# Three spacers that move a two-layer hybrid decoder's matmul operands to multiples of 128 bytes

## The chip, the cores and the metric

The program runs on one core of a Trainium2 chip, in one launch. The metric is device time in microseconds (us): the median of several executions. A partition is one of the 128 rows of the core's on-chip memory; a tile takes the same range of bytes in each of its partitions, and "position" below means the address of a tile's first byte in a partition, modulo 128.

## The reference

Two decoder layers over 256 tokens of 2048 channels. Each layer normalises and modulates its input, multiplies it with one wide matrix, feeds three mixers (a forgetting attention, a sparse attention, a state-space scan), gates and projects each of them, and adds up:

```python
u = rms_norm(x, norm_w) * (1.0 + scale[:, None, :]) + shift[:, None, :]
proj = jnp.dot(u, w_in)                       # 2048 x 18776 columns
...
merged = (gates[:, :, 0] * jnp.dot(y_fox, w_o_fox)
          + gates[:, :, 1] * jnp.dot(y_dsa, w_o_dsa)
          + gates[:, :, 2] * jnp.dot(y_ssd, w_o_ssd))
out = jnp.dot(merged, w_out)
return x + gate[:, None, :] * out
```

Shift, scale and gate come from a product of a second input `c` with `w_ada` (2048 x 6144 for each layer). Everything is float32.

## The kernel before

Weights come in halves of 128 x 1024 float32 (0.5 MB, one transfer of the SP queue into one of seven buffers `raw`). Of each half ScalarE makes a high part `wh` (L175, type float32r) and VectorE the rest `wl` (L176). Activations are split in the same way: `uh` and `ul` are the normalised input, `yh0`, `yl0`, `yh1`, `yl1` the two attentions' outputs, `ysh` and `ysl` the state-space mixer's, `mh` and `ml` the merged sum. Each product of two matrices is then three float32r products into one PSUM bank: high by high, low by high, high by low.

There are two shapes. In `feat` (L213 to L215) a 128 x 128 block of weights is stationary and 256 tokens of an activation stream past it: 256 columns to a product, and new stationary weights for each. In `tok_half` (L180 to L182) 128 tokens are stationary and 512 columns of weights stream past: 15 blocks in each layer, 8 halves a block, 12 products a half, 2880 in all.

TensorE runs in the order in which the program emits its products, so the order is the source's. A clock of ticks, one at each half, places the mixers' small products (plain float32: logits, transposes with `ident`, state-space sums) between the large ones. The first layer starts with ten blocks in `tok_half` form while the modulation `w_ada` is loaded and reduced on VectorE (L229); more of `w_ada` is loaded later beside the other weights, by tick.

Each tile is put by a pool that fills a partition from one end: `const`, `wp` (`raw`, `wh`, `wl`), `up` (`uh`, `ul`), `small`, then the mixers' pools stand one behind the other from the left; `yp`, and what is opened behind it (`ysp` with `ysh` and `ysl`), come from the right end. Sizes are rounded up to 32 bytes. In the built programs this gives these addresses in a partition (modulo 128 in brackets; the two modulo 256 behind the slash):

```
tile          before                 after
wh (first)    65248 (96) / 224       65280 (0) / 0
wl (first)    81632 (96) / 224       81664 (0) / 0
uh            93920 (96) / 224       93952 (0) / 0
ul           110304 (96) / 224      110336 (0) / 0
yh0, mh      137120 (32) / 160      137216 (0) / 0
ml           153504 (32) / 160      153600 (0) / 0
ysh          174944 (96) /  96      174848 (0) / 0
ysl          191328 (96) /  96      191232 (0) / 0
raw (first)   36576 (96) / 224       36608 (0) / 0
qT, kT              (32)                   (0)
dqT, dkT            (96)                   (0)
crep          16512  (0)             16544 (32)
ones, ident         (64)                  (96)
```

All buffers of `wh`, `wl` and `raw` lie 4096 bytes apart, and the blocks inside a tile 512, 1024 or 2048 bytes, so that each operand of a large product starts at its tile's position.

Of the kernel before, what the change touches and what calls it, by code (L numbers as in the profile page):

```python
# [10 lines left out]
F32 = mybir.dt.float32  # L11
# [5 lines left out]
PSUM = bass.MemoryType.PSUM  # L17
# [5 lines left out]
BIG = -1e30  # L23
# [32 lines left out]
# modulation: (layer, blocks, first tick, ticks a tile)  # L56
ADA = ((0, range(8, 12), 212, 1.8), (1, range(8), 270, 1.9), (1, range(8, 12), 600, 4.0))
# start: steps by which the modulation runs ahead of its use, loads of x after which a tile of it is loaded
AHEAD, EARLY = 1, (1,)
# ticks between dependent products of a mixer, by layer  # L60
# [9 lines left out]
class Net:  # L70
    def __init__(self, ctx, tc, xT, c, pos, inv, par, w_ada, w_tm, w_ts, w_sm, w_od, outT):
        self.tc, self.nc = tc, tc.nc
        self.xT, self.c, self.pos, self.inv, self.par = xT, c, pos, inv, par
        self.w_ada, self.w_tm, self.w_ts, self.w_sm, self.w_od, self.outT = w_ada, w_tm, w_ts, w_sm, w_od, outT
        pool = lambda **k: ctx.enter_context(tc.tile_pool(**k))
        self.const = pool(name="const", bufs=1)
        self.wp = pool(name="wp", bufs=1)
        self.up = pool(name="up", bufs=1)
        self.small = pool(name="small", bufs=1)
        self.mm = pool(name="mm", bufs=4, space=PSUM)  # L80
        self.mx = pool(name="mx", bufs=4, space=PSUM)
        self.dram = pool(name="dram", bufs=1, space=DRAM)
        self.ada_queue = []
        self.front = -1000000
        self.nticks = 0
        self.lanes = [[], [], []]
        # TensorE issues in emission order: ticks place the mixers' products between the projections'
        ctx.enter_context(tc.manual_schedule(engines={mybir.EngineType.PE}))

# [21 lines left out]
    def spawn(self, n, gen, *after):  # L111
        """queue a mixer's steps; it starts when the jobs it follows have been emitted"""
        job = Layer()
        job.gen, job.after, job.done = gen, after, False
        self.lanes[n].append(job)
        return job
# [17 lines left out]
    @contextmanager  # L134
    def first(self):
        """what the weights' stream needs goes before everything else, in its own order"""
        tc = self.tc
        outer, tc.cur_priority = tc.cur_priority, self.front
        yield
        self.front, tc.cur_priority = tc.cur_priority, outer  # L140
# [4 lines left out]
    def rsqrt(self, out, ss, scale, eps, tag):  # L145
        """out = (ss * scale + eps) ** -0.5"""
        nc = self.nc
        shape = list(ss.shape)
        x, y, t = [self.st(shape, tag + n) for n in ("_x", "_y", "_t")]
        i = t.bitcast(I32)  # L150
        nc.vector.tensor_scalar(x, ss, scale, eps, op0=OP.mult, op1=OP.add)
        nc.vector.tensor_scalar(i, x.bitcast(I32), 1, None, op0=OP.logical_shift_right)
        nc.vector.tensor_scalar(y.bitcast(I32), i, -1, 0x5F3759DF, op0=OP.mult, op1=OP.add)
        for n in range(3):
            nc.vector.tensor_mul(t, y, y)
            nc.vector.scalar_tensor_tensor(t, t, -0.5, x, op0=OP.mult, op1=OP.mult)
            nc.vector.scalar_tensor_tensor(out if n == 2 else y, t, 1.5, y, op0=OP.add, op1=OP.mult)

# [6 lines left out]
    def half(self, src):  # L165
        """half a piece, as high and low parts"""
        with self.first():
            r = self.raw(src)
            h = self.wp.tile([P, 1024], F32R, tag="wh", name="wh", bufs=NWH)
            l = self.wp.tile([P, 1024], F32R, tag="wl", name="wl", bufs=NWL)  # L170
            self.split(h, l, r)
        return h, l
# [11 lines left out]
    def tok_half(self, out, src, k, k0, k1):  # L184
        """two k tiles x 512 columns, activations stationary"""
        h, l = self.half(src)
        for i in range(2):
            c = slice(i * 512, i * 512 + 512)
            for th in range(2):
                s = slice(th * P, th * P + P)  # L190
                self.three(out[th], self.uh[:, k + i, s], self.ul[:, k + i, s], h[:, c], l[:, c], k + i == k0, k + i == k1)

    def tok_group(self, blocks):
        """out[b][th] is a bank [token, 512 columns]"""
        out = [[self.mmbank() for _ in range(2)] for _ in blocks]
        for k in range(0, KT, 2):
            for b, blk in enumerate(blocks):
                src = self.w_tm[self.l, blk, k // 2]
                self.tok_half(out[b], src, k, 0, KT - 1)
                self.tick()  # L200
        return out

    def feat(self, src, ah=None, al=None, nk=KT):
        """weights stationary: a bank half [128 columns, 256 tokens]"""
# [16 lines left out]
    def ada_raw(self, l, blk, n, r=None):  # L221
        """modulation: half of the sum for the feature tile blk * 4 + n // 2; after every second tile the pair is put together"""
# [35 lines left out]
    def load(self, x, ssq, *tmp):  # L258
        """what the first products wait for: silu of c on all partitions, x and its sum of squares"""
# [97 lines left out]
    def rstd_row(self, ssq):  # L357
        """1 / rms of each token, along the free axis of every partition"""
        nc = self.nc
        ps = self.pbank()  # L360
        for th in range(2):
            nc.tensor.matmul(ps[:, th:th + 1], lhsT=ssq[:, th * P:th * P + P], rhs=self.ones[:, :1], start=True, stop=True)
        rs = self.st([P, 2], "rsu")
        self.rsqrt(rs, ps[:, :2], 1.0 / DM, EPS, "nu")
        pr = self.pbank()
        for th in range(2):
            nc.tensor.matmul(pr[:, th * P:th * P + P], lhsT=rs[:, th:th + 1].to_broadcast([P, P]), rhs=self.ident, start=True, stop=True)
        return pr
# [5 lines left out]
    def u_tile(self, l, k, t):  # L374
        """u = x * A * rstd + shift, as high and low parts"""
# [13 lines left out]
    def start(self, blocks, x, ssq, row, raws, got):  # L389
        """first layer: the modulation arrives by pairs of feature tiles; the first products over each four tiles  # L390
        run as soon as their part of u is there, and add up in SBUF (those of the first two blocks in PSUM)"""
# [64 lines left out]
    def head_rstd(self, t, nh, pool):  # L456
        """1 / rms of each head of t [token, 2, nh * 128]"""
# [11 lines left out]
    def to_heads(self, dst, h0, t, c0, scale=None):  # L469
        """two 128-column blocks of token-major t -> dst[:, h0:h0+2, tokens]"""  # L470
# [11 lines left out]
    def rope(self, v, half, c0, pool):  # L482
        """v [token, 2, heads, dims]: rotate the first 2 * half dims"""
# [32 lines left out]
    def g_small(self, ps, sm, dtt, par, lay, D, pool):  # L516
        """softplus of sdt, log sigmoid of ff, their cumulative sums"""
# [33 lines left out]
        # forget gate: cumulative sums, token-major and as rows (those of the keys)  # L551
# [7 lines left out]
        # state-space decays: cumulative sums by chunk, token-major and as rows  # L559
# [18 lines left out]
    def g_heads(self, n, logits, vals, dst, pool):  # L578
        """causal attention, a head a tick: logits, then softmax and its transpose, then the product with the values"""
# [73 lines left out]
    def g_index(self, iqT, ikT, sm, acc, pool):  # L653
        """scores of the indexer; acc becomes 0 at the selected causal keys and BIG elsewhere"""
# [50 lines left out]
    def gate_y(self, name, y, pool):  # L705
        """y *= 2 * silu(gate); y came with a factor of a half"""
# [10 lines left out]
    def layer(self, l):  # L717
# [3 lines left out]
        # right: y of the attentions, temporaries of both; left: one mixer's operands  # L721
# [13 lines left out]
        D.Fq = yp.tile([P, 2, 8], F32, name="Fq")  # L735
        vp, close_v = self.pool("vp", "left")
# [12 lines left out]
        if l == 0:  # L749
            # x lies where the transposed heads come later  # L750
# [3 lines left out]
        def got(name, j=0, t=None):  # L754
            """a block of projections is there, token-major: the next steps of its mixer"""
# [5 lines left out]
            elif name == "iq":  # L761
                # indexer queries, transposed, lie where the attention's output comes later
# [138 lines left out]
    def conv(self, f, dst, sp):  # L901
        """causal depthwise convolution over 128 channels, then SiLU"""
# [112 lines left out]
    def g_norm(self, l, g, gates, y, sp, S):  # L1015
        """gate and group norm, transposed"""
# [42 lines left out]
def _ada_raws(w):  # L1059
    """w [2048, 6144] by feature tile and half of k, transposed"""  # L1060
# [3 lines left out]
def _pack(i):  # L1064
# [12 lines left out]
    # halves [128, 1024] of pieces: two k tiles x 512 columns, or eight k tiles x 128 columns  # L1077
# [29 lines left out]
```

## Time and profile before

| what | value |
|---|---|
| three timed runs | 2459.23, 2460.9, 2467.44 us; median 2460.9 |
| span of the profiled execution (its own time) | 2465.1 us, 4.2 us over the median |
| TensorE busy | 2418.5 us, 98% of the span, 17256 products |
| VectorE, ScalarE busy | 1752.3 us (71%), 1195.9 us (49%) |
| read from HBM | 520.74 MB, 213 GB/s over the span |
| mean granted TensorE clock | 0.997 |

A product's time in the trace is modelled at its end, so that the times of neighbours overlap: one that is shown with 0.28 us may be followed 0.12 us later by the next. What a product costs in a dense stretch is the step from its start to the next one's start, and that is what the timeline's first column gives. The granted clock is 1.00 where TensorE runs at its upper level, 2.4 GHz.

### The profile page before, as it was taken

How to read it: one execution, taken by the hardware profiler on the slowest of the kernel's cores; microseconds unless marked ns; L12 is line 12 of the kernel's file. 1: busy time of each engine (PE TensorE's matmuls, PEld its weight loads, DVE VectorE, ACT ScalarE, POOL GpSimd, SP SyncE). 2: the span in 40 equal slices, each digit the busy share in tenths (PEclk: the TensorE clock that was granted, in tenths of full speed). 3: DMA queues.
4: the chain of work that ended last, by engine and by line, in shares of the span. 5: the costliest groups of instructions: out<-in, count | busy, mean ns of one | idle time of the engine just before them, and what ended most of it. 6: DMA issues, size and time to landing. Idle time of an engine off the chain costs nothing.

```text
span 2465.1 us, 43733 instructions
## 1 busy us (share of the span) xinstructions
PE 2418.5 (98%) x17256; PEld 2247.5 (91%) x17256; DVE 1752.3 (71%) x3109; ACT 1195.9 (49%) x1932; POOL 1.8 (0%) x11
## 2 busy tenths in 40 slices
PE   6999999999999999999989999999999999999999
PEld 4778799998899999999978877999999999999999
DVE  8899978777766777776775567767776655666554
ACT  4535656555544444343344655555555444444443
POOL 0000000000000000000000000000000000000000
PEclk9999999999999999999999999999999999999999
DMA  9998434544468888788865544544544667776564
GB/s 341 331 328 290 146 120 138 161 157 159 157 214 281 289 281 288 271 276 269 306 205 184 188 138 146 177 152 153 161 155 162 227 229 238 231 233 229 187 214 155
DMA packets 145216, 527.79 MB, mean 214 GB/s; under 512 B 16369, under 2 KB 16881, under 8 KB 145009
## 3 DMA queue, kind: packets, MB, share of 16 engines
q1 hardware_dynamic: 145010, 525.00, 63.4%
q8 instruction: 135, 2.21, 0.4%
q14 instruction: 71, 0.58, 0.1%
HBM read 520.74 MB, written 4.19 MB: 213 GB/s over the span
## 4 chain that ended last, share of the span: by engine, by line
PE 89%; DVE 5%; DMA 4%; issue 1%; ACT 0%; SPq 0%; DVEq 0%
PE pm L213 19%; PE pm L215 19%; PE pm L214 19%; PE pm L180 8%; PE pm L182 8%; PE pm L181 8%; DMA raw<-w_ada 3%; DVE wl L176 2%; DVE raw L229 2%; PE px L987 1%; PE px L475 1%; PE px L609 1%; PE px L996 1%; DMA raw<-w_od 1%; PE held L181 0%
## 5 line engine op out<-in xcount | busy, mean ns | idle before, releaser
L175 ACT CAST wh<-raw 128x1024 fp32r<-128x1024 f32 x788 | 825.4, 1050 | 1002.0 <-PE pm L214 547.5
L176 DVE TENSOR_TENSOR wl<-raw,wh 128x1024 fp32r<-128x1024 f32 x788 | 959.9, 1222 | 344.1 <-PE pm L215 152.9
L213 PE MATMUL pm<-uh,wh 128*128 128x256 f32 x2848 | 816.5, 287 | 0.0
L215 PE MATMUL pm<-uh,wl 128*128 128x256 f32 x2848 | 805.7, 283 | 1.1 <-DVE wl L176 1.1
L214 PE MATMUL pm<-ul,wh 128*128 128x256 f32 x2848 | 805.0, 283 | 0.0
L213 PEld LDWEIGHTS pm<-uh,wh 128*128 128x128 f32 x2848 | 545.1, 191 | 5.2 <-issue 3.9
L214 PEld LDWEIGHTS pm<-ul,wh 128*128 128x128 f32 x2848 | 545.3, 191 | 2.1 <-issue 1.9
L215 PEld LDWEIGHTS pm<-uh,wl 128*128 128x128 f32 x2848 | 545.1, 191 | 1.6 <-DVE wl L176 1.5
L180 PE MATMUL pm<-wh,uh 128*128 128x512 f32 x896 | 361.1, 403 | 1.1 <-ACT uh L378 1.1
L182 PE MATMUL pm<-wl,uh 128*128 128x512 f32 x896 | 352.1, 393 | 6.9 <-DVE wl L176 6.8
L229 DVE SCALAR_TENSOR_TENSOR raw<-raw,crep 128x1024 f32<-128x1024 f32 x192 | 234.0, 1223 | 174.8 <-DMA raw<-w_ada 174.8
L181 PE MATMUL pm<-wh,ul 128*128 128x512 f32 x896 | 350.7, 391 | 0.0
L182 PEld LDWEIGHTS pm<-wl,uh 128*128 128x128 f32 x896 | 169.0, 189 | 46.2 <-DVE wl L176 10.2
L180 PEld LDWEIGHTS pm<-wh,uh 128*128 128x128 f32 x896 | 169.1, 189 | 39.9 <-issue 3.0
L181 PEld LDWEIGHTS pm<-wh,ul 128*128 128x128 f32 x896 | 169.3, 189 | 35.3 <-issue 1.9
L215 PE MATMUL pm<-mh,wl 128*128 128x256 f32 x512 | 142.5, 278 | 5.2 <-DVE wl L176 4.9
L215 PE MATMUL pm<-ysh,wl 128*128 128x256 f32 x512 | 144.7, 283 | 1.2 <-DVE wl L176 1.2
L214 PE MATMUL pm<-ysl,wh 128*128 128x256 f32 x512 | 144.2, 282 | 0.0
L213 PE MATMUL pm<-ysh,wh 128*128 128x256 f32 x512 | 144.1, 281 | 0.0
L214 PE MATMUL pm<-ml,wh 128*128 128x256 f32 x512 | 141.6, 277 | 1.4 <-DVE ml L176 1.4
L213 PE MATMUL pm<-yh,wh 128*128 128x256 f32 x512 | 142.0, 277 | 0.0
L214 PE MATMUL pm<-yl,wh 128*128 128x256 f32 x512 | 141.8, 277 | 0.0
(315 smaller groups left out, 2814.9 us busy)
## 6 DMA issues: line engine op xcount, KB each, us to landing
raw<-w_ts SPq DMA_DIRECT2D x352, 512.0 KB, 3.9
raw<-w_tm SPq DMA_DIRECT2D x240, 512.0 KB, 3.6
raw<-w_ada SPq DMA_DIRECT2D x192, 512.0 KB, 4.6
raw<-w_od SPq DMA_DIRECT2D x192, 512.0 KB, 4.5
raw<-w_sm SPq DMA_DIRECT2D x4, 512.0 KB, 4.7
xr<-xT SPq DMA_DIRECT2D x4, 512.0 KB, 7.0
x<-xn SPq DMA_DIRECT2D x4, 512.0 KB, 6.4
xr<-x SPq DMA_DIRECT2D x4, 512.0 KB, 6.1
```

Of the source, the lines that this page charges most:

```text
L175: self.nc.scalar.copy(h, src)
L176: self.nc.vector.tensor_sub(l, src, h.bitcast(F32))
L180: mm(ps, lhsT=ah, rhs=bh, start=start, stop=False)
L181: mm(ps, lhsT=al, rhs=bh, start=False, stop=False)
L182: mm(ps, lhsT=ah, rhs=bl, start=False, stop=stop)
L213: mm(ps, lhsT=h[:, c], rhs=ah[:, k, :], start=k == 0, stop=False)
L214: mm(ps, lhsT=h[:, c], rhs=al[:, k, :], start=False, stop=False)
L215: mm(ps, lhsT=l[:, c], rhs=ah[:, k, :], start=False, stop=k == nk - 1)
L229: nc.vector.scalar_tensor_tensor(r, r, 0.5, self.crep[:, n % 2 * 1024:n % 2 * 1024 + 1024], op0=OP.mult, op1=OP.mult, accum_out=m.part[:, ...
L475: nc.tensor.transpose(ps[:, j * SEQ + th * P:j * SEQ + th * P + P], t[:, th, c0 + j * P:c0 + j * P + P], self.ident)
L609: nc.tensor.matmul(po[:, :SEQ], lhsT=v[:, 0], rhs=pT[:, :SEQ], start=True, stop=False)
L987: nc.tensor.matmul(pd[:, c * 256 + o % 256:c * 256 + o % 256 + 64], lhsT=dec[:, i, c, :], rhs=xd[:, c, o:o + 64], start=True, stop=True)
```

## The change

Before `wp` a spacer of 32 bytes is put into `const`, which moves everything that stands behind it on the left (weights, `uh`, `ul`, and with a second spacer of 64 bytes in `small` all the mixers' pools). A spacer of 96 bytes at the end of `yp` moves what comes from the right. Each spacer is a tile that GpSimd sets to zero once, so that it is allocated; nothing reads it. The rest of the diff takes comments out of the source and moves line numbers (the function `half` and the products have the same text).

```diff
         self.const = pool(name="const", bufs=1)
+        self.pad(self.const, 32)
         self.wp = pool(name="wp", bufs=1)
         self.up = pool(name="up", bufs=1)
         self.small = pool(name="small", bufs=1)
+        self.pad(self.small, 64)
...
+    def pad(self, pool, nbytes):
+
+        t = pool.tile([P, nbytes // 4], F32, name="pad")
+        self.nc.gpsimd.memset(t, 0.0)
...
         D.Fq = yp.tile([P, 2, 8], F32, name="Fq")
+        self.pad(yp, 96)
```

The order of instructions on TensorE, ScalarE and the SP queue is the same. On GpSimd, at the start of the program, these rows stood before (`ident` is the unit matrix for the transposes, `logf` a table of the forgetting attention):

```order
masks.py:197 MEMSET ident 128x128
L544 MEMSET logf 128x80
masks.py:199 ISA
masks.py:199 AFFINE_SELECT ident<-ident 128x128
L299 AFFINE_SELECT tri<-tri 128x128
L304 AFFINE_SELECT msk<-msk 128x128 x2
L544 MEMSET logf 128x80
```

And these stand there now:

```order
masks.py:197 MEMSET ident 128x128
L128 MEMSET pad 128x8
L128 MEMSET pad 128x16
L128 MEMSET pad 128x24
L551 MEMSET logf 128x80
masks.py:199 ISA
masks.py:199 AFFINE_SELECT ident<-ident 128x128
L306 AFFINE_SELECT tri<-tri 128x128
L311 AFFINE_SELECT msk<-msk 128x128 x2
L128 MEMSET pad 128x24
L551 MEMSET logf 128x80
```

Three settings of a spacer now stand ahead of the one that finishes `ident`, and a fourth, that of the second layer's `yp`, ahead of the second layer's `logf`. On VectorE two small copies of `ident` into `hot` change places with one scaling, all within the first set-up.

## Rows read from the trace of the kernel before

**Rows 1.** The page: busy time of each engine, and the transfers' share in slices.

```profile
PE 2418.5 (98%) x17256; PEld 2247.5 (91%) x17256; DVE 1752.3 (71%) x3109; ACT 1195.9 (49%) x1932; POOL 1.8 (0%) x11
DMA  9998434544468888788865544544544667776564
```

**Rows 2.** The page: the chain that ended last, by engine.

```profile
PE 89%; DVE 5%; DMA 4%; issue 1%; ACT 0%; SPq 0%; DVEq 0%
```

**Rows 3.** The page: groups of large products, moving operand first; busy, mean, idle before.

```profile
L213 PE MATMUL pm<-uh,wh 128*128 128x256 f32 x2848 | 816.5, 287 | 0.0
...
L180 PE MATMUL pm<-wh,uh 128*128 128x512 f32 x896 | 361.1, 403 | 1.1 <-ACT uh L378 1.1
...
L213 PE MATMUL pm<-yh,wh 128*128 128x256 f32 x512 | 142.0, 277 | 0.0
```

**Rows 4.** Timeline of TensorE, `uh` and `ul` moving: start, duration, instruction.

```profile
710.77 0.28 PE L214 MATMUL pm<-ul,wh 128*128 128x256 f32 x1
...
711.85 0.28 PE L214 MATMUL pm<-ul,wh 128*128 128x256 f32 x1
```

**Rows 5.** The same view, `yh` and `yl`, then `mh` and `ml` moving.

```profile
705.29 0.28 PE L215 MATMUL pm<-yh,wl 128*128 128x256 f32 x1
...
706.32 0.28 PE L215 MATMUL pm<-yh,wl 128*128 128x256 f32 x1
...
2399.76 0.28 PE L214 MATMUL pm<-ml,wh 128*128 128x256 f32 x1
...
2400.89 0.28 PE L215 MATMUL pm<-mh,wl 128*128 128x256 f32 x1
```

**Rows 6.** The same view, `ysh` and `ysl` moving.

```profile
2197.78 0.28 PE L214 MATMUL pm<-ysl,wh 128*128 128x256 f32 x1
...
2198.85 0.28 PE L214 MATMUL pm<-ysl,wh 128*128 128x256 f32 x1
```

**Rows 7.** The same view, 512 columns of weights moving.

```profile
1319.79 0.39 PE L181 MATMUL pm<-wh,ul 128*128 128x512 f32 x1
...
1320.70 0.39 PE L182 MATMUL pm<-wl,uh 128*128 128x512 f32 x1
```

**Rows 8.** Groups by shape: two plain float32 products of 256 columns.

```profile
L626 PE MATMUL px<-kT,qT 128*128 128x256 f32 x32 | 9.6, 380 | 0.0
L700 PE MATMUL px<-dkT,dqT 128*128 128x256 f32 x32 | 9.6, 380 | 0.0
```

**Rows 9.** The chain about 244 us: start, length, what.

```profile
244.40 0.87 PE px L475 x8
```

**Rows 10.** Windows: length, busy of each engine, granted clock, DMA share, GB/s.

```profile
30.00:210.00 180.00, 172.47 (x730) 139.46 (x731) 166.59 (x271) 77.23 (x94) 0.00 (x0) 0.99 0.92 328
...
700.00:1025.00 325.00, 325.00 (x2752) 324.78 (x2751) 232.29 (x332) 138.96 (x161) 0.00 (x0) 1.00 0.82 277
1025.00:1255.00 230.00, 221.12 (x1851) 217.76 (x1850) 167.06 (x262) 91.62 (x115) 0.00 (x0) 1.00 0.84 282
...
1900.00:2465.00 565.00, 562.03 (x4779) 561.83 (x4777) 329.14 (x413) 236.08 (x272) 0.00 (x0) 1.00 0.65 215
```

**Rows 11.** Waits of TensorE: in total, times, longest.

```profile
PE pm L215 <- DVE wl L176: 7.1, 10, 2.1
PE pm L182 <- DVE wl L176: 6.8, 5, 1.9
```

**Rows 12.** The chain from 1095 to 1135 us.

```profile
1096.19 5.80 DMA raw<-w_ada
...
1103.27 4.33 DMA raw<-w_ada
...
1108.89 4.65 DMA raw<-w_ada
```

**Rows 13.** Groups by shape: two VectorE operations, and one setting on GpSimd.

```profile
L176 DVE TENSOR_TENSOR wl<-raw,wh 128x1024 fp32r<-128x1024 f32 x788 | 959.9, 1222 | 344.1 <-PE pm L215 152.9 <-PE pm L182 112.5 <-issue 61.2
...
L229 DVE SCALAR_TENSOR_TENSOR raw<-raw,crep 128x1024 f32<-128x1024 f32 x192 | 234.0, 1223 | 174.8 <-DMA raw<-w_ada 174.8
...
L544 POOL MEMSET logf<- 128x80 f32 x2 | 0.3, 166 | 264.3 <-PE px L558 264.3
```

## The prediction

> **What bounds the kernel now.** I read the page's busy times first: TensorE is busy 98% of the span, VectorE 71% [rows 1]. The chain that ended last agrees: 89% of it is TensorE, 5% VectorE, 4% transfers [rows 2]. So nearly all of the time is the number of products times the step from one to the next, and the view that counts is the timeline's column of starts.
>
> There the steps differ by the moving tile, although shape, type and granted clock (1.00, the level of 2.4 GHz) are the same. Ten starts with `uh` and `ul` span 1.08 us: 120.0 ns a product [rows 4]. With `yh` and `yl` nine steps take 1.03 us, 114.4 ns; with `mh` and `ml` ten take 1.13 us, 113.0 ns [rows 5]. With `ysh` and `ysl` nine take 1.07 us, 118.9 ns [rows 6]. Where 512 columns of weights stream, four steps take 0.91 us, 227.5 ns [rows 7]. One column per clock would be 256 / 2.4 = 106.7 ns and 512 / 2.4 = 213.3 ns. The excess is thus some 13 ns for `uh`, as much for 512 columns (14), 12 for `ysh`, and 6 to 8 for `yh` and `mh`. It is paid per product, not per column.
>
> Against the table of addresses: what costs 12 to 14 ns more starts 96 bytes into its 128, what costs 6 to 8 starts 32 bytes into it. Two stretches are not TensorE's alone: up to about 230 us transfers run at 328 GB/s and a share of 0.92 with VectorE busy 166.59 of 180 us, and from 1025 to 1255 us (282 GB/s) TensorE has gaps [rows 10].
>
> **The change part by part.** *Price of an aligned product.* No row has one. Along the line from 96 bytes (120.0) through 32 bytes (mean of 114.4 and 113.0: 113.7) position 0 is at 113.7 - (120.0 - 113.7) / 2 = 110.5 ns; by `mh` alone it is 109.5. I take 110. The lower bound is 106.7, the upper the best step seen, 113.0. Each product also loads 128 columns of weights: eight transposes, each with such a load, take 0.87 us, 108.75 ns each [rows 9], so loads come fast enough for 110. For 512 columns I take the same 10 ns off, 217.5, between 213.3 and 220.5.
>
> The Trainium skill has a price for a warm stream, in "TensorE: Matmul & The Clock Gate", section "Back-to-back issue gap": columns over 2.4 plus 2.5 ns, 109.2 and 215.8 here. No stretch of this trace shows it, and by it the sum below would be 144 us instead of 130.
>
> *The sum.* `uh` and `ul`: 3 x 2848 products [rows 3] x 10.0 = 85.4 us. `ysh` and `ysl`: 3 x 512 x 8.9 = 13.7 (the groups of `ysh`, `yh` and `mh` all have 512). `yh`: 1536 x 4.4 = 6.8; `mh`: 1536 x 3.0 = 4.6. Products of 512 columns: 2880 by the listing, less the 960 of the ten starting blocks, 1920 x 10.0 = 19.2. Together 129.7 us. With the lower bounds: 13.3 x 8544 + 12.2 x 1536 + 7.7 x 1536 + 6.3 x 1536 + 14.2 x 1920 ns = 181 us; with the upper ones: 7.0 x 8544 + 5.9 x 1536 + 1.4 x 1536 + 7.0 x 1920 ns = 85 us.
>
> *What does not become shorter.* The starting blocks I give nothing: 960 x 10 ns would be 9.6 us, but there transfers and VectorE set the pace [rows 10]. If transfers gained from their new places in `raw`, VectorE's 166.59 of 180 us would leave 13 us at most; the trace shows no transfer to another position of `raw`, so I take nothing.
>
> From 1025 to 1255 us the chain goes through one transfer of `w_ada` after another (5.80, 4.33 and 4.65 us within 20 us [rows 12]). The potential in it is about 530 products of `uh` x 10.0 + 530 of `ysh` x 8.9 + 768 of `mh` x 3.0 ns = 12.3 us (1851 products in that window [rows 10], split by the order of the source); as TensorE is still busy 221 of 230 us there, I take half of it off, 6 us. Between 700 and 1025 us transfers have a share of 0.82 at 277 GB/s; a step shorter by a fifteenth makes that 0.88, under the 0.92 of the start, so the gain holds. From 1900 us on the share is 0.65 and nothing is near [rows 10].
>
> TensorE waits for `wl` 15 times for 13.9 us [rows 11]; with weights used up faster a wait of 2 us can come more often, 4 us off. What is late next is VectorE's split: 1222 ns a half against 24 x 110 ns = 2.6 us, with its other work 71% of the span before and about 75% after.
>
> *Moved positions with no price.* `ident` and `ones` go from 64 to 96. Plain float32 products take no notice: `kT` at 32 and `dkT` at 96 both show 380 ns [rows 8]. Nor does VectorE: `crep` at 0 and `wh` at 96 as second operand give 1223 and 1222 ns [rows 13]. The four settings of spacers are shorter than the 166 ns of `logf` [rows 13], and GpSimd is busy 1.8 us in all [rows 1]. The three ahead of `ident` delay it by at most 0.5 us, hidden behind the loading of `x`; without that cover they would cost those 0.5 us.
>
> So 129.7 - 6 - 4 = 119.7 us off the profiled execution's 2465.1: 2345. That execution was 4.2 us over the median of its runs, so 2341 for a median.
>
> **The rivals.**
>
> *Weights set the step.* Each product of 256 columns also brings in 128 columns of weights, whose tile is at 96 in every row of the trace. If the 113.0 ns of `mh` is what such a load takes wherever it starts, the 256-column terms stop at the upper bound: 59.8 + 9.1 + 2.2 = 71 us, plus 19.2 for 512 columns, less 7 = 83 us, 2378. For it: 113.0 is the least step of that shape. Against it: the 108.75 ns of the transposes [rows 9].
>
> *The two operands' places to each other (slower).* The trace also fits another reading. Modulo 256, `uh` lies where `wh` lies (difference 0, 120.0 ns), `ysh` 128 away (118.9), `yh` and `mh` 64 away on the other side (114.4, 113.0). If a stream of weights and a moving stream disturb each other most when their places agree, the change makes all of them agree: `uh` stays, and `yh` pays 5.6 x 1536 = 8.6 us, `mh` 7.0 x 768 = 5.4 us (the first layer's half lies in the stretch of transfers), `ysh` 1.1 x 1536 = 1.7 us. That is 15.7 us more, 2477. It decides once `yh` and `mh` lose 3.2 ns a product (2304 x 3.2 ns = 7.4 us) and `uh` gains nothing. For it: `uh` and `ysh` share a position but not a step. Against it: 512 columns pay the same 14 ns although a load of 128 columns is over early in them.
>
> *Position is not the cause (no change).* `uh` lies next to the weights (65 to 127 thousand bytes into the partition), `yh`, `mh` and `ysh` beyond 137 thousand. If that, and not the position in 128 bytes, makes the step, everything stays: 2461. For it: `uh`, the nearest, is the dearest. Against it: `ysh`, the farthest, is nearly as dear.
>
> The Trainium skill speaks for this rival in "SBUF — State Buffer", "Specifications (TRN2)": memory lines are 16 bytes, and a penalty falls on crossing to a new one with too few hits. By that rule nothing would change, since every tile starts at a multiple of 32 before and after; the trace agrees only in part, as `uh` and `mh` both do so and differ by 7 ns.
>
> **How the numbers follow.** Chances: position in 128 bytes 0.55 (2341, its own range 2290 to 2384 from the bounds 181 - 10 and 85 - 8, less the 4.2); weights set the step 0.12 (2378); no change 0.14 (2461); slower 0.19 (2477). The first reading gets most because one rule covers both shapes and all four tiles to within 2 ns; the third fits 256 columns as well, but not the 512. A measurement of this kernel can tell about 0.3% from no change, 7.4 us. Faster by more: 0.55 + 0.12 = 0.67; slower 0.19; same 0.14. The range goes from the first case's lower bound, 2290, up over the case of no change to 2466, which leaves out the slower case, 0.19.
>
> **What would show it.** In the profile after, the timeline's steps: `uh`, `ysh`, `yh` and `mh` all at one value, 110 ns, and 217 ns for 512 columns, say the first reading is right. 113 ns for all and 217 say that weights set the step. 120 ns for all, `yh` and `mh` included, say it is the two operands' agreement. Steps unchanged tile by tile say that position is not the cause. If the steps fall and the time does not, the page's idle before L180, L182 and L215 must have grown by as much, with `wl` or transfers of `raw` as releasers, above all before 230 us and from 1025 to 1255 us. The forecast goes wrong most in the first term: each nanosecond of `uh` is 8.5 us.

## The result, and the profile after

The changed kernel is slower: a median of 2479.23 us (2477.14 to 2479.51) beside 2463.22 us for the kernel before on the same chip, a ratio of 1.0064 with an interval of 1.0049 to 1.0078. The forecast was 2341; the rival "the two operands' places to each other" had said 2477. The profiled execution took 2477.14 us with a span of 2475.4, 10.3 us longer than the span before.

From the page after: busy times with their share of the span, the 40 slices of transfers, the chain that ended last, and the group of `uh`. The products are now in L220 to L222 (`feat`) and L187 to L189 (`tok_half`), the split in L182 and L183.

```profile
PE 2433.1 (98%) x17256; PEld 2266.0 (92%) x17256; DVE 1755.9 (71%) x3109; ACT 1197.4 (48%) x1932; POOL 1.9 (0%) x15
...
DMA  9998444555568888888855544545445777777564
...
PE 91%; DVE 5%; DMA 3%; issue 1%; ACT 0%; SPq 0%; DVEq 0%
...
L220 PE MATMUL pm<-uh,wh 128*128 128x256 f32 x2848 | 817.0, 287 | 0.0
```

The counts of products, the vector work and the transfers are those of before; TensorE alone is longer. The group of `uh` has the mean that it had [rows 3], 287 ns, so the loss lies with other tiles. The starts in the timeline show it (first column: start in us; the first and last row of four dense stretches):

```profile
711.81 0.28 PE L220 MATMUL pm<-yh,wh 128*128 128x256 f32 x1
...
713.49 0.28 PE L222 MATMUL pm<-yh,wl 128*128 128x256 f32 x1
...
1321.74 0.39 PE L189 MATMUL pm<-wl,uh 128*128 128x512 f32 x1
...
1323.79 0.39 PE L189 MATMUL pm<-wl,uh 128*128 128x512 f32 x1
...
2209.79 0.28 PE L220 MATMUL pm<-uh,wh 128*128 128x256 f32 x1
...
2210.99 0.28 PE L221 MATMUL pm<-ul,wh 128*128 128x256 f32 x1
...
2398.31 0.28 PE L222 MATMUL pm<-mh,wl 128*128 128x256 f32 x1
...
2399.63 0.28 PE L221 MATMUL pm<-ml,wh 128*128 128x256 f32 x1
```

`yh`: 14 steps in 1.68 us, 120.0 ns, where it had 114.4 [rows 5]. `mh`: 11 steps in 1.32 us, 120.0, where it had 113.0 [rows 5]. `uh`: 10 steps in 1.20 us, 120.0 as before [rows 4]. 512 columns: 9 steps in 2.05 us, 227.8, as before [rows 7]. Summed over the whole trace from start to start (each product until the next one starts, the last one left out), the products with `yh` and `yl` went from 175.6 to 184.2 us (+8.6), `mh` and `ml` from 186.4 to 191.9 (+5.5), `ysh` and `ysl` from 184.9 to 184.3, `uh` and `ul` in `feat` from 1037.1 to 1036.6, the 512-column products from 687.4 to 684.5, the rest of TensorE from 187.6 to 187.8. These sum to +10.3 us, the whole difference of the spans.

TensorE's waits after (us in total, times, longest), and the windows (length, busy time of TensorE, weight loads, VectorE, ScalarE and GpSimd, granted clock, DMA share, GB/s):

```profile
PE pm L189 <- DVE wl L183: 7.5, 5, 1.9
PE pm L222 <- DVE wl L183: 3.3, 3, 1.6
```

```profile
30.00:210.00 180.00, 171.65 (x735) 138.68 (x736) 168.04 (x274) 78.29 (x94) 0.00 (x0) 1.00 0.93 332
1030.00:1260.00 230.00, 222.36 (x1842) 221.10 (x1841) 167.37 (x270) 93.52 (x116) 0.00 (x0) 1.00 0.85 284
1905.00:2475.00 570.00, 567.38 (x4729) 567.18 (x4727) 326.17 (x409) 233.42 (x269) 0.00 (x0) 1.00 0.66 211
```

Slower products wait less for `wl`: 8 times for 10.8 us, where [rows 11] has 13.9. The first stretch is as it was [rows 10], and the clock was granted at its upper level throughout, so neither transfers nor the clock made the loss. From 1905 us on VectorE is busy 326 of 570 us and ScalarE 233, yet all 2303 steps of `yh`, `ysh` and `mh` there are 120 ns: what slows them does not come and go with those engines' work.

### The profile page after: what moved, and what is told of

Its sections match the earlier page's. It is cut to its first block, busy times and chain, and to the rows that moved or that the text cites. A ratio compares the mean times of both kernels' runs of the same rounds, so it can differ in the third digit from the quotient of the medians.

```text
span 2475.4 us, 43737 instructions
## 1 busy us (share of the span) xinstructions
PE 2433.1 (98%) x17256; PEld 2266.0 (92%) x17256; DVE 1755.9 (71%) x3109; ACT 1197.4 (48%) x1932; POOL 1.9 (0%) x15
## 4 chain that ended last, share of the span: by engine, by line
PE 91%; DVE 5%; DMA 3%; issue 1%; ACT 0%; SPq 0%; DVEq 0%
PE pm L220 20%; PE pm L222 20%; PE pm L221 20%; PE pm L187 8%; PE pm L189 8%; PE pm L188 8%; DVE raw L236 2%; DMA raw<-w_ada 2%; DVE wl L183 2%; PE px L995 1%; DMA raw<-w_od 1%; PE px L482 1%; PE px L616 1%; PE px L1004 1%; PE px L608 0%
## 5 line engine op out<-in xcount | busy, mean ns | idle before, releaser
L182 ACT CAST wh<-raw 128x1024 fp32r<-128x1024 f32 x788 | 826.1, 1050 | 1041.4 <-PE pm L221 568.9
L183 DVE TENSOR_TENSOR wl<-raw,wh 128x1024 fp32r<-128x1024 f32 x788 | 961.3, 1222 | 360.8 <-PE pm L222 162.8
L220 PE MATMUL pm<-uh,wh 128*128 128x256 f32 x2848 | 817.0, 287 | 0.0
L222 PE MATMUL pm<-uh,wl 128*128 128x256 f32 x2848 | 805.6, 283 | 0.0
L220 PEld LDWEIGHTS pm<-uh,wh 128*128 128x128 f32 x2848 | 546.0, 192 | 5.2 <-issue 3.9
L222 PEld LDWEIGHTS pm<-uh,wl 128*128 128x128 f32 x2848 | 546.0, 192 | 0.0
L187 PE MATMUL pm<-wh,uh 128*128 128x512 f32 x896 | 360.3, 402 | 1.1 <-ACT uh L385 1.1
L189 PE MATMUL pm<-wl,uh 128*128 128x512 f32 x896 | 351.1, 392 | 7.6 <-DVE wl L183 7.5
L189 PEld LDWEIGHTS pm<-wl,uh 128*128 128x128 f32 x896 | 168.6, 188 | 46.7 <-DVE wl L183 10.9
L187 PEld LDWEIGHTS pm<-wh,uh 128*128 128x128 f32 x896 | 168.8, 188 | 39.5 <-issue 3.0
L222 PE MATMUL pm<-mh,wl 128*128 128x256 f32 x512 | 145.3, 284 | 3.3 <-DVE wl L183 3.3
L220 PE MATMUL pm<-yh,wh 128*128 128x256 f32 x512 | 144.9, 283 | 0.0
L222 PE MATMUL pm<-yh,wl 128*128 128x256 f32 x512 | 144.9, 283 | 0.0
L220 PE MATMUL pm<-ysh,wh 128*128 128x256 f32 x512 | 144.9, 283 | 0.0
```

What stands on the lines that cost most here:

```text
L182: self.nc.scalar.copy(h, src)
L183: self.nc.vector.tensor_sub(l, src, h.bitcast(F32))
L187: mm(ps, lhsT=ah, rhs=bh, start=start, stop=False)
L189: mm(ps, lhsT=ah, rhs=bl, start=False, stop=stop)
L220: mm(ps, lhsT=h[:, c], rhs=ah[:, k, :], start=k == 0, stop=False)
L222: mm(ps, lhsT=l[:, c], rhs=ah[:, k, :], start=False, stop=k == nk - 1)
```

## The experiments

Places below are modulo 256, and a **difference** is the moving operand's place less the weights' place (modulo 256). All edits are to the changed kernel. Where one time is given without an interval, the kernel ran once. Steps without a line beside them are means over a tile's steps of under 130 ns (longer ones hold a wait), for the second layer, from start to start in the trace.

**e1_mixed: every activation at another place.** Weights stay at 0, `uh` goes to 64, `yh0` to 32, `yh1` to 96, `ysh` to 160, `mh` to 224.

```diff
+        self.pad(self.up, 64)
-        self.pad(self.small, 64)
...
+                self.pad(ysp, 96)
+        self.pad(hp, 32)
...
+                self.pad(mp, 224)
```

> Weights stay at 0 modulo 256 as in the changed kernel; each activation gets another place: uh, ul at 64, yh0, yl0 at 32, yh1, yl1 at 96, ysh, ysl at 160, mh, ml at 224. Theory of the difference (the step of a 256-column product follows from moving place minus weights' place, modulo 256): five differences that no run has shown, each with a step of its own between 107 and 120 ns, and 160 need not be 113. Theory of the own place (the moving tile's place alone): ysh at 160 gives the 113 to 114 ns that yh and mh gave there before, mh at 224 the 120 ns that uh gave there. Theory that the spacers did something else: uh stays at 120 wherever it lies. Products of 512 columns stay at 227 ns by all three, unless the place of their stationary uh counts.

Measured: 2465.36 us, beside 2464.14 of before. Steps: `yh0` (difference 32) 116.6 ns, `uh` (64) 117.8, `yh1` (96) 120.0 (single steps alternate between 115 and 125), `ysh` (160) 117.4, `mh` (224) 118.3. `ysh` at 160 has the place at which `mh` took 113.0 before [rows 5], yet takes 117.4: a tile's own place does not set its step. The timeline of this kernel also shows the weights as the moving side (first and last of a stretch):

```profile
1324.64 0.40 PE L188 MATMUL pm<-wh,ul 128*128 128x512 f32 x1
...
1326.97 0.40 PE L189 MATMUL pm<-wl,uh 128*128 128x512 f32 x1
```

Ten steps in 2.33 us are 233 ns, where the weights had the same place and 227.8 ns in the kernel after. Only the stationary `uh` has moved, so 512 columns too depend on both operands.

**e2_all160: everything together at another place.** All operands agree again, but at 160.

```diff
-        self.pad(self.const, 32)
+        self.pad(self.const, 192)
...
-        self.pad(yp, 96)
+        self.pad(yp, 192)
```

> Weights and all activations at 160 modulo 256, the place at which yh and mh had 113 to 114 ns before, but with no difference between weights and activations. Theory of the difference: 120 ns for uh, ysh, yh and mh alike, and the time of the changed kernel, 2479 us. Theory of the own place: 113.5 ns for all of them, 6.5 x 8544 + 6.5 x 4608 ns = 85 us less, about 2394 us.

Measured: 2477.86 us. The timeline with `mh`:

```profile
2398.28 0.28 PE L222 MATMUL pm<-mh,wl 128*128 128x256 f32 x1
...
2399.61 0.28 PE L221 MATMUL pm<-ml,wh 128*128 128x256 f32 x1
```

11 steps in 1.33 us are 121 ns by the two decimals; the mean for each of `uh`, `yh`, `ysh` and `mh` is 120.0, as at place 0. Position 0 has nothing of its own; agreement has.

**e3_w32_a224: the cheap difference for all.** Before, `yh` and `mh` had difference 192. Here weights are at 32 and every activation at 224.

```diff
-        self.pad(self.const, 32)
+        self.pad(self.const, 64)
...
+        self.pad(self.up, 192)
...
-        self.pad(yp, 96)
+        self.pad(yp, 128)
```

> All activations at 224 modulo 256, the place at which uh had 120 ns before, and the weights at 32: the difference is 192, that of yh and mh before. Theory of the difference: 113.5 ns for uh, ysh, yh and mh alike; against before 6.5 x 8544 + 5.4 x 1536 ns = 64 us less, some 6 us of it lost where transfers are on the chain, so 2405 us (2395 to 2420). Theory of the own place: 120 ns for all of them, 2479 us as with the change.

Measured: 2428.37 us (2425.48 to 2430.24), a ratio to before of 0.9856 with an interval of 0.9841 to 0.9871: the fastest kernel of the study that does the whole work. Its timeline with `uh`, its waits, and its stretch of many transfers:

```profile
2199.84 0.28 PE L221 MATMUL pm<-uh,wh 128*128 128x256 f32 x1
...
2201.20 0.28 PE L221 MATMUL pm<-uh,wh 128*128 128x256 f32 x1
```

```profile
PE pm L223 <- DVE wl L184: 12.6, 17, 3.2
...
PE pm L190 <- DVE wl L184: 6.8, 5, 1.8
```

```profile
1020.00:1245.00 225.00, 213.05 (x1801) 209.77 (x1799) 164.76 (x260) 91.04 (x115) 0.00 (x0) 0.98 0.84 285
```

12 steps in 1.36 us are 113.3 ns, for the same `uh` that took 120.0. It even has the place that it had before (224); the weights have moved, by 64 bytes. The gain is 36 us, where about 59 were expected (64, less 6 lost beside transfers). All steps in `feat` of under 130 ns went from 13003 with a mean of 118.3 ns (before, 1537.8 us) to 12945 with 114.3 (1479.3 us), 58.5 us less: `uh` does not hold 113 everywhere. Three quarters of these short steps are 113 or 114 ns, from 1900 us on nearly all of them; but between 300 and 700 us and between 1500 and 1900 us, where small products of the mixers stand between, a good part runs at 117 to 119. The steps of 130 ns and more, those with waits, went from 148 with 46.2 us to 206 with 65.8, 19.6 us more (58 steps have passed from the one group to the other). The 512-column products took 2.3 us more (687.4 to 689.7). -58.5 + 19.6 + 2.3 = -36.6 us, the difference of the spans (2465.1 and 2428.5). The waits for `wl` grew as the prediction had feared, to 22 times for 19.4 us [rows 11 for before].

**e4_no_small: one spacer out.** Without the spacer in `small`, `yh` and `mh` have difference 192 again; `uh` and `ysh` stay at 0.

```diff
-        self.pad(self.small, 64)
```

> The changed kernel without its spacer of 64 bytes in small: yh and mh lie 192 past the weights (modulo 256) as before the change, uh and ysh at 0 as with it. Theory of the difference: yh and mh back at 113 to 114 ns, uh and ysh at 120; the time of before plus 1.7 us for ysh, about 2465 us. Theory of the own place: yh and mh are at 192, where no run has been, uh and ysh stay at 120, so between 2463 and 2479 us. If the loss comes from another spacer (settings on GpSimd, moved constants), 2479 us with yh and mh at 113.

Measured: 2464.74 us over 10 runs, a ratio of 1.0006 (0.9996 to 1.0015): no change. The timeline with `mh`:

```profile
2398.30 0.28 PE L219 MATMUL pm<-mh,wh 128*128 128x256 f32 x1
...
2399.54 0.28 PE L221 MATMUL pm<-mh,wl 128*128 128x256 f32 x1
```

11 steps in 1.24 us, 112.7 ns by the two decimals; the mean is 113.4. The whole loss of the change hangs on this one spacer of 64 bytes. It moves the mixers' other tiles too, but in the trace of the changed kernel only `yh`, `yl`, `mh` and `ml` had lost.

**e5_wl_apart: whose partner?** In e3's placement `wl` alone is moved to the activations' place, to see whether a product's step goes by its own weights or by those loaded during it.

```diff
         (in half, ahead of the first wl tile)
+            if not hasattr(self, "apart"):
+                self.apart = self.pad(self.wp, 192) or 1
```

> The faster placement (activations at 224, wh at 32) with wl alone moved to 224: wh still differs by 192, wl by 0. A product of the three takes the step from its start to the next one's. Theory that the moving stream meets the load of the next product's weights: only the second of the three, ul by wh, runs beside a load of wl; its step is 120 ns, those of the first (uh by wh) and the third (uh by wl) stay at 113 ns. Theory that a product pays for its own pair of operands: the third, uh by wl, has 120 ns, the other two 113. Theory that only the place of wh counts: 113 for all three, as before this edit. Either of the first two gives a mean of 115 to 116 ns and about 2440 us.

Measured: 2463.96 us; none of the three theories had that. The three products of a block take nearly the same:

```profile
2398.24 0.28 PE L222 MATMUL pm<-mh,wh 128*128 128x256 f32 x1
...
2399.53 0.28 PE L224 MATMUL pm<-mh,wl 128*128 128x256 f32 x1
```

11 steps in 1.29 us, 117.3 ns; over the second layer's `mh` the three take 117.6, 118.3 and 117.4. One of three products in a bad relation costs all three. Whether the partner is the weights in use or the weights being loaded stays open.

**e6_fine and e7_fine2: steps of 8 and 16 bytes.** In e3's placement the tiles are allocated 256 bytes larger and used from an offset (`yh0`, `yh1`, `mh`, `ysh`; e6: 16, 240, 8, 248 bytes; e7: 48, 208, 176, 112).

```diff
+    def at(self, pool, name, k, off):
+        t = pool.tile([P, k * SEQ + 64], F32R, name=name)
+        return t[:, off // 4:off // 4 + k * SEQ].rearrange("p (k s) -> p k s", s=SEQ)
...
-                mh = mp.tile([P, KT, SEQ], F32R, name="mh")
+                mh = self.at(mp, "mh", KT, 8)
```

> The faster placement with differences about 192 in smaller steps: yh0, yl0 at 208, yh1, yl1 at 176, mh, ml at 200, ysh, ysl at 184; uh, ul stay at 192. The theory of the difference says that each has a step of its own and uh keeps 113 ns; it names no best value. If the step is made by lines of 64 bytes or more, 8 and 16 bytes change nothing and all stay at 113; if the difference counts byte by byte, steps between 107 and 120 ns. For the time this is one look: 2425 to 2445 us.

> The same with yh0, yl0 at 240, yh1, yl1 at 144, mh, ml at 112, ysh, ysl at 48. Together with the looks before, this gives the step at differences of 0, 32, 48, 64, 96, 112, 128, 144, 160, 176, 184, 192, 200, 208, 224 and 240. The theory of the difference expects a map that falls from 120 at 0 and rises back to it, with its lowest place near 192; the theory that only agreement (0) costs expects 113 to 114 at all four. Time 2425 to 2450 us.

Measured: 2446.12 and 2440.68 us, beside 2466.3 of before. In e6 the differences 208 and 176 give 119 ns, 184 and 200 give 120 (the lines show `ysh` at 184, then `mh` at 200):

```profile
2199.82 0.28 PE L226 MATMUL pm<-ysh,wh 128*128 128x256 f32 x1
...
2201.14 0.28 PE L228 MATMUL pm<-ysh,wl 128*128 128x256 f32 x1
...
2397.98 0.28 PE L226 MATMUL pm<-mh,wh 128*128 128x256 f32 x1
...
2399.78 0.28 PE L226 MATMUL pm<-mh,wh 128*128 128x256 f32 x1
```

11 steps in 1.32 us, and 15 in 1.80. Eight bytes off 192 to either side, and the step is 120 again; `uh`, left at 192, has 113.6. The tiles at 184 and 200 are also the only ones of all runs that start 8 bytes off a multiple of 16, which may be a part of their price; 16 bytes off 192 (176 and 208) there is no such doubt. At 200 the three products of a block differ: 119, 125 and 116 ns. In e7, 240 gives 117.0, 48 gives 118.3, and two new low ones appear: 113.7 at 144 and 113.4 at 112. So neither a map that falls from 0 to one lowest place nor a price for agreement alone fits.

**e8_all112 and e9_all144: those two for every tile.** `uh` and `ul` share one tile that is used from byte 16; the spacers are set to match.

```diff
-        self.uh = self.up.tile([P, KT, SEQ], F32R, tag="uh", name="uh")
-        self.ul = self.up.tile([P, KT, SEQ], F32R, tag="ul", name="ul")
+        u = self.up.tile([P, 2 * KT * SEQ + 8], F32R, tag="uh", name="uh")
...
+                mh = self.at(mp, "mh", KT, 176)
```

> All activations 112 bytes past the weights (modulo 256), the place at which mh held 113 ns from the 5th to the 95th of 100 products in a look. If the step depends on the difference alone, uh, ysh, yh and mh take 113 ns here too, and 2425 to 2435 us as at 192; if uh falls into that step sooner after the small products of the mixers than at 192 (its mean there was 115 to 116 ns between 400 and 700 us), 2415 to 2425 us. Own place: uh at 144 is new and gives no number.

> The same with 144 bytes, where yh1 held 113 to 114 ns. Difference alone: 113 to 114 ns for all, 2425 to 2440 us. Products of 512 columns see the opposite difference (weights move, uh stands) and may take 227 to 233 ns, up to 6 us in all.

Measured: 2436.68 us (ratio 0.9888, 0.9871 to 0.9904) and 2473.91 us (1.0041, 1.0026 to 1.0056). At 112 the 256-column products do better than in e3 (`uh` sums to 991.5 us, e3 998.6), but the 512-column ones, whose operands have the same relation the other way round, pay for it (700.8 us, before 687.4):

```profile
1324.73 0.39 PE L194 MATMUL pm<-wh,uh 128*128 128x512 f32 x1
...
1326.83 0.39 PE L194 MATMUL pm<-wh,uh 128*128 128x512 f32 x1
```

Nine steps in 2.10 us, 233 ns. At 144 nothing held 113; `ysh` in e9:

```profile
2199.30 0.28 PE L226 MATMUL pm<-ysh,wh 128*128 128x256 f32 x1
...
2201.20 0.28 PE L227 MATMUL pm<-ysl,wh 128*128 128x256 f32 x1
```

16 steps in 1.90 us, 118.8 ns (over all, 118.7), at the difference that gave 113.7 in e7. So the difference alone does not fix the step.

**e10_half_load_after and e11_half_load_w32: shorter weight loads.** Two of three products load and use 64 columns of weights (and change places), so the low parts are left out of the sum for the other 64 channels; e10 in the placement of the change, e11 in that of e3.

```diff
-            mm(ps, lhsT=h[:, c], rhs=al[:, k, :], start=False, stop=False)
-            mm(ps, lhsT=l[:, c], rhs=ah[:, k, :], start=False, stop=k == nk - 1)
+            n = P if k == nk - 1 else 64
+            d = slice(c.start, c.start + n)
+            mm(ps[:64], lhsT=l[:, c.start:c.start + 64], rhs=ah[:, k, :], start=False, stop=False)
+            mm(ps[:n], lhsT=h[:, d], rhs=al[:, k, :], start=False, stop=k == nk - 1)
```

> The changed kernel (all differences 0), but of the three products of each block two load only 64 of the 128 columns of weights and give half of the output channels: low by high and, except for the last block of a sum, high by low. So the low parts are left out of the sum for the other 64 channels; 256 columns still move in each product. Theory that the moving stream pays for the load that runs beside it: a load of half the length costs half as much or less, so the mean of the three steps falls from 120 to 112 to 115 ns. Theory that the moving stream pays by its own lines: 120 ns for all three, unchanged. The time then is about 2430 us or 2477 us.

> The same halved loads in the faster placement (difference 192, 113 ns). If the 113 ns still hold a part for loads, the mean falls to 108 to 111 ns and the time to some 2400 us; if 113 ns is what 256 moving columns take, it stays at 113 and near 2428 us.

Measured: 2447.29 us, 32 less than the changed kernel, and 2427.79 us, as e3. The timeline with `mh` in e10:

```profile
2398.32 0.28 PE L223 MATMUL pm<-mh,wl 128*64 128x256 f32 x1
...
2399.60 0.28 PE L220 MATMUL pm<-mh,wh 128*128 128x256 f32 x1
```

And in e11:

```profile
2398.29 0.28 PE L221 MATMUL pm<-mh,wh 128*128 128x256 f32 x1
...
2399.54 0.28 PE L225 MATMUL pm<-ml,wh 128*64 128x256 f32 x1
```

11 steps in 1.28 us, 116.4 ns instead of 120.0; and 11 in 1.25 us, 113.6. The means are 116.7 and 113.3, the latter the same as with whole loads. What is above 113.3 shrinks with the edit: two of three loads halved take away half of it (3.3 of 6.7 ns). The edit also halves the rows that those products write, so that this goes with the load beside the moving stream is likely, not shown by itself; that the excess follows the places of weights and activations, and the results' place was left alone, speaks for the load. 113.3 does not shrink, so neither loads nor rows written set it. Both theories of the expectation for e10 had named another number (120, or 112 to 115); it lies between.

**e12_carry: difference 144 in company.** `uh` at 192, all others at 144.

```diff
+        self.pad(self.up, 192)
...
+            yh = self.at(hp, f"yh{n}", 8, (208, 208)[n])
...
+                mh = self.at(mp, "mh", KT, 208)
```

> uh and ul 192 bytes past the weights, all other activations 144 bytes past them (modulo 256). At 144 two looks disagree: yh1 held 113 to 114 ns where uh lay at 192, and 118.6 ns where all lay at 144. Theory of the difference alone: the step at 144 is 118 to 119 ns for yh, ysh and mh, as where all lay there. Theory that the streams keep the phase in which they enter: yh and ysh, which take turns with uh in groups of 24 and 48 products, take over its 113 ns; mh, 768 in a row behind them, keeps it too or falls to 118 after the first wait.

Measured: 2439.93 us, beside 2463.25 of before. The timeline with `mh`:

```profile
2397.93 0.28 PE L226 MATMUL pm<-mh,wh 128*128 128x256 f32 x1
...
2399.63 0.28 PE L226 MATMUL pm<-mh,wh 128*128 128x256 f32 x1
```

15 steps in 1.70 us, 113.3 ns, and so through all 768 products of the second layer's `mh`. The same tile at the same address, with the weights at theirs, took 118.7 in e9, where `uh` was at 144 too; only `uh` has moved between the two kernels. Within e12 the first layer's `mh` takes 117.5. And the theory that the others take over 113 ns from `uh` does not fit, since `uh`, at 192, itself runs at 117.8 ns from 1950 us on, beside `ysh` at 113.3:

```profile
2314.67 0.28 PE L226 MATMUL pm<-uh,wh 128*128 128x256 f32 x1
...
2320.33 0.28 PE L226 MATMUL pm<-ysh,wh 128*128 128x256 f32 x1
...
2325.77 0.28 PE L226 MATMUL pm<-uh,wh 128*128 128x256 f32 x1
```

48 steps of `uh` in 5.66 us are 117.9 ns, 48 of `ysh` in 5.44 us 113.3. So one difference can have two steps, 192 as well as 144, and what else runs in the kernel has a part in which one is held; what it is that decides was not found.

All steps of 256 columns, by difference:

| difference | step, ns | difference | step, ns |
|---|---|---|---|
| 0 | 120.0 | 144 | 113.3 (e12, `mh`), 113.7 (e7), 118.7 (e9) |
| 32 | 116.6 | 160 | 117.4 |
| 48 | 118.3 | 176 | 119.2 |
| 64 | 117.8 | 184 | 120.1 |
| 96 | 120.0 | 192 | 113.3 (e3), 117.8 (e12, `uh`) |
| 112 | 113.4 (e7), 113.3 (e8) | 200, 208 | 120.0, 119.3 |
| 128 [rows 6] | 118.8 | 224, 240 | 118.3, 117.0 |

## Why the prediction was wrong

**What bounds the kernel: right.** Steps of TensorE's products account for the whole change of the span, here and in e3.

**Price of an aligned product: the step that failed.** The prediction drew a line from 96 bytes (120.0 ns) through 32 (113.7) to 0 (110.5) and took 110, for a term of 85.4 us on `uh` alone. The term came out at 0.5 us. The line had two points and the wrong variable: `uh` and `mh` differed in position modulo 128 and also in their difference to the weights, and the trace held both readings, as the rival said. The runs showed the second: the step goes with the two operands' places to each other, and `uh`, which stayed at difference 0, stayed at 120.0. e2 (agreement at 160: 120) and e3 (difference 192: 113.3, at other places than before) tell them apart. The other terms, 13.7, 6.8, 4.6 and 19.2 us, rested on the same line: 0.6 us was gained on `ysh`, 8.6 and 5.5 lost on `yh` and `mh`, 2.9 gained on 512 columns.

**The slower rival, at a chance of 0.19: right in place, and in price for `yh` and `mh`.** It had 8.6 + 5.4 + 1.7 = 15.7 us; the trace shows 8.6, 5.5 and -0.6. Of the 5.5, 5.0 are the second layer's, as it had said. The dense step of `ysh` did rise, from 118.8 to 120.0, but eleven long steps of before, 3.8 us in all, did not come again. That the medians differ by 16.0, so near to 15.7, is partly luck: the two traces differ by 10.3. Its point of decision, 3.2 ns on `yh` and `mh`, was passed with 5.6 and 7.0. What had been held against it was misjudged: that 512 columns pay as much although a load ends early in them. They depend on the partner too, 227.8 ns at difference 0 and 233 in e1 and e8, only with another sign: of the placements tried, agreement is their cheapest. As a full rule it is too simple: for 256 columns agreement is among the dearest, but 96, 184 and 200 cost as much, the distance does not order the rest (192 takes 113.3), and one difference can have two steps.

**Weights set the step: refuted.** It had 113 ns for all tiles, and after the change all have 120.0; halved loads leave 113.3 where it is (e11).

**Position is not the cause: refuted.** In e3 and e4 tiles are moved by some tens to hundreds of bytes within the same region, and steps change by 7 ns. The rule that spoke for it, in the Trainium skill's "SBUF — State Buffer", "Specifications (TRN2)" (memory lines of 16 bytes, a penalty on crossing them), would have given no change; the measurement differs: all tiles of after and of e3 start at multiples of 32, and take 120.0 and 113.3.

**What does not become shorter: right in kind.** In the change nothing became shorter, so its 10 us off were not put to the test. In e3, where 58.5 us came off the short steps, 19.6 came back in long ones, waits for `wl` among them (13.9 to 19.4 us): a larger part than the 10 of 129.7.

**Moved positions with no price: right.** The spacers' settings, from the page after:

```profile
L128 POOL MEMSET pad<- 128x24 f32 (+2 forms) x4 | 0.3, 112 | 0.0
```

0.3 us on an engine that nobody waits for; the first stretch did not move. The 380 ns that the prediction set side by side [rows 8] are modelled durations and not steps, so they could not have told; but the rest of TensorE's products, these among them, went from 187.6 to 187.8 us.

**From the span to the median: 1.7 us too little.** The prediction set a span beside times, and an execution's time is 1.7 us more than its span (2477.14 and 2475.4 here), so about 6 us were to be taken off and not 4.2. It changes nothing.

**What stays open.** e10 speaks for loads beside the stream as what makes the excess over 113, which would fit two readers of one memory that hinder each other by where their bytes lie; no run shows that memory itself. Which of two loads is the partner of a product, why 112, 144 and 192 can be good, and what picks between the two steps that e9 and e12 show were not settled.

## What to carry to other kernels

Where TensorE is the bound and each product brings new weights, read the step from start to start, tile by tile, and set it beside the *difference* of the two operands' addresses, not beside each address: round addresses for all may be the worst choice (2479 us, the slowest kernel here), spacers that set the two operands apart the best (2428, the fastest that does the whole work). When the trace of before fits two variables equally, a line through two points of one of them is no price; a kernel that moves all operands together and one that moves one alone tell them apart in two runs. And a placement is a measured choice: a difference that is good in one stretch may not be held in another, so try it on the whole kernel.

## What was not expected of the hardware

A product of 256 columns at the same granted clock takes 113.3 to 120.1 ns by where its operands lie, and 16 bytes can make the difference (192: 113.3; 176 and 208: 119.2 and 119.3). No placement brought a dense stretch under 113. The difference does not tell all: the same tile at the same addresses held 113.3 or 118.7 ns (`mh` in e12 and e9), and in e12 113.3 in one layer and 117.5 in the other. As far as seen the places act with a period of 256 bytes: modulo 512 `uh` and `mh` lie 0 and 256 from the weights after the change, and both take 120.0; in e3 they lie 192 and 448 away, and both take 113.3. And the gap that the Trainium skill gives for warm products ("TensorE: Matmul & The Clock Gate", "Back-to-back issue gap": columns over 2.4 plus 2.5 ns, by estimate 109.2 ns for 256 columns) is under every dense stretch of large products that these runs show. The section calls it the gap of an isolated product and says that in a stream the loads of weights set the spacing too, so it is not the price of such a stream, which the prediction took it for.
